# The order of the mixer's steps: a gated pair of products ahead of the first query products, the gates one product later

## The chip, the cores and the metric

One NeuronCore of a Trainium2 chip. The metric is the device time of one execution in microseconds, the median of several. TensorE (PE) does the matrix products, PEld are its weight loads, VectorE (DVE), ScalarE (ACT) and GpSimd (POOL) the elementwise work, and SyncE (SP) starts the transfers from HBM. Each engine takes its instructions from one queue in the order of the program.

## What is computed

Two layers of a decoder trunk on 512 tokens of 1024 features. Each has a mixer and an MLP, both with a conditioned normalisation ahead of them, and a normalised, gated residual behind them. The mixer, from the reference, shortened:

```python
u = h @ w_in
x_m, z, glu_a, glu_b = jnp.split(u, [1024, 2048, 3072], axis=-1)
x_c = silu(causal_depthwise_conv(x_m, w_conv_m, b_conv_m))       # 4 taps
q, k, v = headwise products of x_c, x_c, x_m                      # 4 heads of 256
ig, fg = split(concat(q, k, v) @ w_gates + b_gates)
h_m = mlstm_chunkwise(q, k / 16, v, ig, log_sigmoid(fg))
h_m = sigmoid(z) * group_layer_norm(h_m, 4 heads, g_mh)
a = causal_depthwise_conv(glu_a * sigmoid(glu_b), w_dw, b_dw)     # 31 taps
a = silu(group_layer_norm(a, 8 groups, g_cn, b_cn))
return concat(h_m, a) @ w_out
```

## The kernel before

Activations lie feature by feature: a tile is 128 features by 512 tokens. A float32 product is made of three passes in a reduced format (`passes`, L177 to L179): weight and activation are each split into a high and a low part. A weight block of 128 output features (`wblock`) is 512 KB; SP loads it, ScalarE casts the high part (L169), GpSimd subtracts for the low part (L170), and `gemm` makes 24 products of 512 columns from it into one of three PSUM banks "mm".

The mixer is written as steps, which `mixer` calls in the order of a string, `ORDERS[l]` for layer `l`:

- `Xh`: the two blocks of x_m of head h (`xm_proj`), and `Vh`, its 4-tap convolution and swish (`xm_conv`: ScalarE L525, L529, GpSimd L530, VectorE L533, then a cast L155 on ScalarE and a subtraction L156 on GpSimd). There is one buffer for the convolved tile.
- `Qh`: query, key and value products of head h (three blocks of 12 products; queries and keys read what `Vh` left), the transposes of the values (L567), and the head's share of the gates (six products L578, summed by VectorE at L583).
- `Gi`: gated tile i, two blocks (glu_b, then glu_a), ScalarE's tanh and VectorE's L438. Tiles 0 to 2 are made ahead of the string.
- `E`: the gates. Two products L591, L592 read the sum; a chain on ScalarE and VectorE (L601 to L612, scans L610 and L620, L622) follows, and its results are transposed on TensorE (L625, then L626) and spread into columns (L631, L636, L640).
- `Zi`: one block for the output gate. `ah`, `bh`, `ch`: scores, weighted sums and output of head h; a starts with a product L647 that spreads the running maximum, then score products L660 and VectorE's L652, L662; sums are L672, transposes L701.
- `Ci`: the 31-tap convolution of tiles 2i and 2i+1 (`conv31`): a first step L427 and 30 steps L429 each on VectorE, accumulating in PSUM. Then `conv_norm`: a copy by ScalarE (L476), four transposes (L479), statistics (L485, L486, L146), a scaling (L490), four transposes back (L494), and L500.
- `Oi`: the output projection's part of the convolved half. `Nj` (layer 0 only): conditioning products (L245, L250).

The string does not set the order on the engines by itself. The framework schedules: it issues ready instructions by priority, where an earlier place in the program counts as higher, and a timing model decides what is ready when. `Ci` stands late in the string, but its steps are issued earlier wherever that model finds VectorE free. The order found is then fixed in the program.

Of the kernel before, what the change touches and what calls it, by code (L numbers as in the profile page):

```python
# [53 lines left out]
def trunk(ctx, tc, xT, vecs, bg, cst, ccol, crow, wadn, wadt, win, win0, wqkv, wgate, wout, wff1, wff2, yT):  # L54
# [8 lines left out]
    ps = ctx.enter_context(tc.tile_pool(name="ps", bufs=1, space=PSUM))  # L63

    NSLOT = 25
    ORDERS = ['X0 G3 V0 X1 Q0 V1 N4 G4 X2 G5 N5 Q1 V2 X3 N6 Q2 V3 G6 Q3 E G7 N7 Z0 Z1 Z2 Z3 N8 a0 Z4 b0 Z5 a1 b1 Z6 N9 c0 C0 a2 Z7 c1 b2 C1 C2 C3 O0 O1 a3 O2 c2 O6 O3 b3 O4 O5 c3 O7', 'X0 V0 G3 X1 Q0 V1 X2 G4 Q1 V2 G5 X3 Q2 V3 G7 Q3 E Z0 G6 Z1 Z2 Z3 a0 Z4 Z5 b0 a1 Z6 b1 Z7 c0 a2 c1 C0 b2 C1 C2 C3 O0 O1 a3 O6 O2 c2 O3 b3 O4 O5 c3 O7']
    WPRI = 300
    NK = 4
    KM = 4
# [345 lines left out]
    def mixer(l, hp, pre):  # L415
# [309 lines left out]
        hm = []  # L725
        for step in ORDERS[l].split():
            i = int(step[1:] or 0)
# [173 lines left out]
```

## Time and profile before

| | us |
|---|---|
| median of three runs (1607.35 to 1611.52) | 1609.53 |
| the profiled execution, its own time | 1608.05 |
| its span | 1606.3 |
| TensorE busy | 1537.6 |
| VectorE busy | 878.1 |
| GpSimd busy | 798.5 |
| ScalarE busy | 688.6 |
| first product of X0, layer 0 (start) | 78.12 |
| first product of Z4, layer 0 | 301.53 |
| first product of Z4, layer 1 | 1064.80 |
| first product of O0, layer 1 | 1121.63 |

Layer 0's mixer begins at some 78 us, behind the conditioning and the first gated tiles; layer 1's at some 876 us. Busy times overlap, since the engines run beside each other; a wait in the profile names the engine and line that ended it. How rows are to be read is said with each group below.

### The profile page before, as it was taken

How to read it: one execution, taken by the hardware profiler on the slowest of the kernel's cores; microseconds unless marked ns; L12 is line 12 of the kernel's file. 1: busy time of each engine (PE TensorE's matmuls, PEld its weight loads, DVE VectorE, ACT ScalarE, POOL GpSimd, SP SyncE). 2: the span in 40 equal slices, each digit the busy share in tenths (PEclk: the TensorE clock that was granted, in tenths of full speed). 3: DMA queues.
4: the chain of work that ended last, by engine and by line, in shares of the span. 5: the costliest groups of instructions: out<-in, count | busy, mean ns of one | idle time of the engine just before them, and what ended most of it. 6: DMA issues, size and time to landing. Idle time of an engine off the chain costs nothing.

```text
span 1606.3 us, 21229 instructions
## 1 busy us (share of the span) xinstructions
PE 1537.6 (96%) x8020; PEld 1255.5 (78%) x8020; DVE 878.1 (55%) x1761; ACT 688.6 (43%) x1168; POOL 798.5 (50%) x488
## 2 busy tenths in 40 slices
PE   4899998999999999999999999999999999999997
PEld 3577665677998888888899777676899888888887
DVE  6399999843164432346747999997326320012114
ACT  3345563453454322332453665544355432233242
POOL 0166662256744444445962877434674444444462
PEclk9999999999999999999999999999999999999999
DMA  8514332413412555556730222220242233222331
GB/s 309 194 53 138 116 131 104 144 53 92 145 53 94 191 187 197 174 194 218 255 116 8 73 79 67 91 79 27 84 141 65 80 95 102 92 92 92 96 127 53
DMA packets 56270, 188.91 MB, mean 118 GB/s; under 512 B 6376, under 2 KB 8552, under 8 KB 56168
## 3 DMA queue, kind: packets, MB, share of 16 engines
q1 hardware_dynamic: 56168, 187.56, 35.2%
q8 instruction: 63, 1.03, 0.3%
q14 instruction: 39, 0.32, 0.1%
HBM read 185.44 MB, written 2.10 MB: 117 GB/s over the span
## 4 chain that ended last, share of the span: by engine, by line
PE 78%; DVE 6%; ACT 2%; POOL 1%; issue 1%; DMA 0%; POOLq 0%; ACTq 0%; DVEq 0%
PE ps_mm L177 23%; PE ps_mm L179 23%; PE ps_mm L178 23%; DVE ps_cv L429 3%; PE ps_mm L672 2%; PE ps_mm L660 2%; PE ps_ax L316 1%; PE ps_ax L245 1%; POOL wlo L170 1%; ACT whi L169 1%; PE ps_ax L578 1%; PE ps_ax L647 0%; DVE csb L490 0%; PE ps_ax L342 0%; PE ps_ax L701 0%
## 5 line engine op out<-in xcount | busy, mean ns | idle before, releaser
L170 POOL TENSOR_TENSOR wlo<-raw,whi 128x1024 fp32r<-128x1024 f32 (+1 forms) x216 | 498.8, 2311 | 565.1 <-ACT whi L169 547.0
L177 PE MATMUL ps_mm<-slot,whi 128*128 128x512 f32 (+1 forms) x1632 | 621.9, 382 | 8.1 <-ACT slot L155 4.9
L179 PE MATMUL ps_mm<-slot,wlo 128*128 128x512 f32 (+1 forms) x1632 | 622.1, 382 | 5.0 <-POOL wlo L170 4.8
L178 PE MATMUL ps_mm<-slot,whi 128*128 128x512 f32 (+1 forms) x1632 | 621.7, 381 | 0.0
L169 ACT CAST whi<-raw 128x1024 fp32r<-128x1024 f32 (+1 forms) x216 | 216.4, 1002 | 498.9 <-PE ps_mm L178 357.7
L177 PEld LDWEIGHTS ps_mm<-slot,whi 128*128 128x128 f32 x1632 | 307.3, 188 | 78.9 <-ACT slot L155 5.6
L179 PEld LDWEIGHTS ps_mm<-slot,wlo 128*128 128x128 f32 x1632 | 307.6, 188 | 73.8 <-issue 6.3
L178 PEld LDWEIGHTS ps_mm<-slot,whi 128*128 128x128 f32 x1632 | 308.0, 189 | 65.6 <-issue 3.8
L429 DVE SCALAR_TENSOR_TENSOR ps_cv<-slot,vv,ps_cv 128x512 f32<-128x512 f32 x480 | 332.9, 747 | 1.5
L767 DVE TENSOR_TENSOR ps_mm<-rl,ps_mm 128x512 f32<-128x512 f32 (+1 forms) x78 | 46.7, 599 | 280.6 <-ACT rl L766 280.5
L177 PE MATMUL ps_mm<-slot 128*128 128x256 f32 (+1 forms) x568 | 158.5, 292 | 14.5 <-DVE slot L769 7.4
L178 PE MATMUL ps_mm<-slot 128*128 128x256 f32 (+1 forms) x568 | 163.2, 290 | 0.3 <-POOL slot L355 0.3
L179 PE MATMUL ps_mm<-slot 128*128 128x256 f32 (+1 forms) x568 | 162.6, 289 | 0.0
L177 PEld LDWEIGHTS ps_mm<-slot 128*128 128x128 f32 x568 | 105.3, 190 | 19.9 <-ACT slot L357 8.4
L179 PEld LDWEIGHTS ps_mm<-slot 128*128 128x128 f32 x568 | 107.8, 190 | 2.2 <-issue 0.8
L178 PEld LDWEIGHTS ps_mm<-slot 128*128 128x128 f32 x568 | 107.6, 190 | 1.9 <-POOL slot L355 0.5
L170 POOL TENSOR_TENSOR slot<-raw,slot 128x1024 fp32r<-128x1024 f32 x34 | 85.2, 2527 | 14.4 <-issue 12.7
L272 DVE CUSTOM_DVE_ANT_0 adr<-adr,cbc,ini 128x1024 f32<-128x1024 f32 x40 | 66.0, 1659 | 23.3 <-DMA adr<-in_wadt 23.3
L147 POOL TENSOR_TENSOR small<-small,mhalf 128x4 f32<-128x4 f32 (+1 forms) x38 | 34.6, 911 | 81.3 <-DVE small L146 76.6
L769 DVE TENSOR_TENSOR slot<-ps_mm,slot 128x512 fp32r<-128x512 f32 (+1 forms) x78 | 46.4, 595 | 38.2 <-ACT slot L768 37.9
L530 POOL TENSOR_TENSOR xa<-xa,s 128x512 f32<-128x512 f32 x48 | 61.9, 1289 | 5.1 <-ACT s L529 1.9
L768 ACT CAST slot<-ps_mm 128x512 fp32r<-128x512 f32 (+1 forms) x78 | 39.8, 510 | 45.9 <-DVE ps_mm L767 45.9
(201 smaller groups left out, 1570.5 us busy)
## 6 DMA issues: line engine op xcount, KB each, us to landing
raw<-in_wff SPq DMA_DIRECT2D x138, 512.0 KB, 3.5
raw<-in_win SPq DMA_DIRECT2D x58, 512.0 KB, 3.3
adr<-in_wadt SPq DMA_DIRECT2D x56, 512.0 KB, 4.5
raw<-in_wout SPq DMA_DIRECT2D x36, 512.0 KB, 3.5
adr<-in_wadn SPq DMA_DIRECT2D x28, 512.0 KB, 4.2
raw<-in_wqkv SPq DMA_DIRECT2D x24, 256.0 KB, 2.6
slot<-in_wadt SPq DMA_DIRECT2D x8, 512.0 KB, 5.1
raw<-in_win SPq DMA_DIRECT2D x8, 384.0 KB, 7.1
```

The lines of the kernel that those rows point to most:

```text
L147: pool.tensor_tensor(y, u, mhalf[:, 0:n], op=ALU.pow)
L169: act.copy(out=r32(hi), in_=raw)
L170: (lo_eng or pool).tensor_tensor(r32(lo), raw, hi, op=ALU.subtract)
L177: pe.matmul(out, whi, xh, start=first, stop=False)
L178: pe.matmul(out, whi, xl, start=False, stop=False)
L179: mark[0] = pe.matmul(out, wlo, xh, start=False, stop=last)
L272: red = dve.tensor_tensor_reduce(raw, raw, cbc, scale, 0.0 if one else ini, ALU.mult, ALU.add, m)
L429: dve.scalar_tensor_tensor(acc, at[i][:, k:k + T], w, acc, op0=ALU.mult, op1=ALU.add)
L530: pool.tensor_tensor(acc, acc, tk, op=ALU.add)
L767: dve.tensor_tensor(o, rl[:, ts], o, op=ALU.mult)
L768: act.copy(out=r32(pr[:, 0, ts]), in_=o)
L769: last[0] = dve.tensor_tensor(r32(pr[:, 1, ts]), o, pr[:, 0, ts], op=ALU.subtract)
```

## The change

Only the two strings change. In both layers G4 now stands ahead of Q0, and the rhythm is X, G, Q, V for every head; G7 is ahead of Q3, and Z0 stands between Q3 and E. In layer 0 the conditioning steps N4 to N7 move one or two places with it; in layer 1 G6, which stood behind Z0, is now ahead of Q2. From Z1 (layer 0) and Z1 (layer 1) on, the strings are as before. The first part of each, cut behind Z3:

```diff
-X0 G3 V0 X1 Q0 V1 N4 G4 X2 G5 N5 Q1 V2 X3 N6 Q2 V3 G6 Q3 E G7 N7 Z0 Z1 Z2 Z3
+X0 G3 V0 X1 G4 Q0 V1 N4 X2 G5 Q1 N5 V2 X3 G6 Q2 N6 V3 G7 Q3 Z0 E N7 Z1 Z2 Z3
...
-X0 V0 G3 X1 Q0 V1 X2 G4 Q1 V2 G5 X3 Q2 V3 G7 Q3 E Z0 G6 Z1 Z2 Z3
+X0 V0 G3 X1 G4 Q0 V1 X2 G5 Q1 V2 X3 G6 Q2 V3 G7 Q3 Z0 E Z1 Z2 Z3
```

What the scheduler makes of it, at three places. First VectorE in layer 0, around the end of the gates' chain. Before, these rows stood there (L622 ends the chain, L500 ends a normalisation, L438 makes gated tile 7, L427 begins the convolution of the eighth tile):

```order
L429 SCALAR_TENSOR_TENSOR ps_cv<-slot,vv,ps_cv 128x512
L622 TENSOR_TENSOR s_1677<-s_1659,ml 4x512
L429 SCALAR_TENSOR_TENSOR ps_cv<-slot,vv,ps_cv 128x512
L500 SCALAR_TENSOR_TENSOR yt<-cth,ps_cx 128x512
L429 SCALAR_TENSOR_TENSOR ps_cv<-slot,vv,ps_cv 128x512
L438 SCALAR_TENSOR_TENSOR slot<-s_1735,ps_mm 128x512
L429 SCALAR_TENSOR_TENSOR ps_cv<-slot,vv,ps_cv 128x512
L427 TENSOR_SCALAR ps_cv<-slot,vv,hgb 128x512
```

Now gated tile 7 (its L438 is two rows further up) and the beginning of the eighth tile stand ahead of the last head's share of the gates (L583), with which the chain begins:

```order
L427 TENSOR_SCALAR ps_cv<-slot,vv,hgb 128x512
L429 SCALAR_TENSOR_TENSOR ps_cv<-slot,vv,ps_cv 128x512 x12
L485 BN_STATS small<-ps_cx 128x6 x4
L429 SCALAR_TENSOR_TENSOR ps_cv<-slot,vv,ps_cv 128x512
L486 BN_AGGR small<-small 128x2 x4
L429 SCALAR_TENSOR_TENSOR ps_cv<-slot,vv,ps_cv 128x512
L146 TENSOR_SCALAR small<-small 128x4
L429 SCALAR_TENSOR_TENSOR ps_cv<-slot,vv,ps_cv 128x512 x2
L490 TENSOR_SCALAR csb<-ps_cx,small 128x128 x4
L429 SCALAR_TENSOR_TENSOR ps_cv<-slot,vv,ps_cv 128x512 x2
L583 TENSOR_TENSOR gsb<-gsb,ps_ax 128x512
```

The eighth tile's first step has moved from behind the chain to ahead of its beginning. Counted over the whole queue from the first L427 of the layer, L427 and L429 stand 209 times ahead of L622 before and 248 times now (layer 1: 186 and 222).

Second, TensorE in layer 0, at the fourth tile's normalisation. Before, the transposes L479 stood among the key products of head 2, with other products up to L494:

```order
L178 MATMUL ps_mm<-slot,whi 128x512
L179 MATMUL ps_mm<-slot,wlo 128x512
L479 MATMUL ps_cx<-cs,csb 128x128 x4
L245 MATMUL ps_ax<-adr,cc 32x512 x2
L177 MATMUL ps_mm<-slot,whi 128x512
```

Now they stand between the two blocks of G6 (L250 belongs to the conditioning), and L494 follows directly:

```order
L179 MATMUL ps_mm<-slot,wlo 128x512
L250 MATMUL ps_ax<-cs,s_1220 128x1 x4
L479 MATMUL ps_cx<-cs,csb 128x128 x4
L494 MATMUL ps_cx<-cs,csb 128x128 x4
L177 MATMUL ps_mm<-slot,whi 128x512
```

The statistics and the scaling on VectorE lie between these two in the data, and no product stands between them any more.

Third, TensorE in layer 1, from the scores of the first head to Z4. Before, L647 and L626 stood among the products of Z1:

```order
L479 MATMUL ps_cx<-cs,csb 128x128 x4
L647 MATMUL ps_ax<-ml,cs 128x512
L179 MATMUL ps_mm<-slot,wlo 128x512
L177 MATMUL ps_mm<-slot,whi 128x512
L178 MATMUL ps_mm<-slot,whi 128x512
```

Now they stand behind Z3, and Z4 (the last row) comes behind the second L647, the last score products of the first head and the transposes of the seventh tile:

```order
L494 MATMUL ps_cx<-cs,csb 128x128 x4
L647 MATMUL ps_ax<-ml,cs 128x512
L626 MATMUL ps_ax<-cs,s_8748 128x4
L625 MATMUL ps_ax<-cs,s_8735 128x4
...
L631 MATMUL ps_ax<-tr,cs 128x16
L647 MATMUL ps_ax<-ml,cs 128x512
L660 MATMUL ps_mm<-slot 128x128 x2
L479 MATMUL ps_cx<-cs,csb 128x128 x4
L177 MATMUL ps_mm<-slot,whi 128x512
```

The blocks Z1 to Z3 are now ahead of L626, and no block of products stands between L626 and Z4.

## Rows read from the trace of the kernel before

**Rows 1.** The page: busy us (share); VectorE's 40 slices in tenths.

```profile
PE 1537.6 (96%) x8020; PEld 1255.5 (78%) x8020; DVE 878.1 (55%) x1761; ACT 688.6 (43%) x1168; POOL 798.5 (50%) x488
...
DVE  6399999843164432346747999997326320012114
```

**Rows 2.** Stretches: us, busy PE, PEld, DVE, ACT, POOL, clock, DMA, GB/s.

```profile
80.00:260.00 180.00, 168.79 (x778) 120.73 (x778) 174.03 (x300) 96.77 (x154) 111.03 (x89) 0.98 0.30 104
...
876.00:1040.00 164.00, 160.39 (x729) 121.74 (x728) 157.64 (x279) 97.99 (x156) 111.29 (x89) 1.00 0.24 76
```

**Rows 3.** VectorE by line, 78 to 270 us: count, busy, mean ns, idle.

```profile
L429 DVE SCALAR_TENSOR_TENSOR ps_cv<-slot,vv,ps_cv 128x512 f32<-128x512 f32 x202 | 138.8, 746 | 0.4
...
L490 DVE TENSOR_SCALAR csb<-ps_cx,small 128x128 f32<-128x128 f32 x24 | 8.1, 397 | 0.0
L485 DVE BATCH_NORM_STATS2 small<-ps_cx 128x6 f32<-128x128 f32 x24 | 5.3, 280 | 1.9 <-PE ps_cx L479 1.9
...
L146 DVE TENSOR_SCALAR small<-small 128x4 f32<-128x4 f32 x6 | 3.5, 586 | 0.0
```

**Rows 4.** VectorE's timeline, layer 0: start us, duration us, line, operation.

```profile
80.39 2.72 DVE L429 SCALAR_TENSOR_TENSOR ps_cv<-slot,vv,ps_cv 128x512 f32<-128x512 f32 x4
...
269.48 0.67 DVE L622 TENSOR_TENSOR s<-s,ml 4x512 f32<-4x512 f32 x1
```

**Rows 5.** Chain of waits, 205 to 262 us: shares by line.

```profile
by line: DVE ps_cv L429 52.9%; PE ps_ax L245 6.2%; issue 4.9%; DVE s L605 4.9%; DVE csb L490 4.5%; DVE xa L533 3.9%; PE ps_mm L179 2.4%; DVE s L610 2.2%; DVE gsb L583 2.1%; PE ps_mm L178 2.1%; DVE yt L500 2.1%; PE ps_mm L177 2.1%; PE ps_ax 
```

**Rows 6.** TensorE's waits, 78 to 356 us: total us, times, longest.

```profile
PE ps_mm L177 <- ACT slot L155: 4.9, 2, 3.5
PE ps_cx L479 <- ACT csb L476: 2.3, 1, 2.3
PE ps_mm L591 <- DVE gsb L583: 1.9, 1, 1.9
PE ps_ax L625 <- DVE s L612: 1.3, 1, 1.3
```

**Rows 7.** The page: subtraction, cast, transfer (us to landing). Timeline: two products.

```profile
L170 POOL TENSOR_TENSOR wlo<-raw,whi 128x1024 fp32r<-128x1024 f32 (+1 forms) x216 | 498.8, 2311 | 565.1 <-ACT whi L169 547.0
...
L169 ACT CAST whi<-raw 128x1024 fp32r<-128x1024 f32 (+1 forms) x216 | 216.4, 1002 | 498.9 <-PE ps_mm L178 357.7
...
raw<-in_win SPq DMA_DIRECT2D x58, 512.0 KB, 3.3
...
1042.12 0.39 PE L178 MATMUL ps_mm<-slot,whi 128*128 128x512 f32 x1
1042.35 0.39 PE L179 MATMUL ps_mm<-slot,wlo 128*128 128x512 f32 x1
```

**Rows 8.** TensorE's timeline, layer 0: first L626, L660, first of Z4.

```profile
277.48 0.22 PE L626 MATMUL ps_ax<-cs,s 4*128 4x4 f32 x1
...
295.37 4.14 PE L660 MATMUL ps_mm<-slot 128*128 128x512 f32 x12
...
301.53 0.50 PE L177 MATMUL ps_mm<-slot,whi 128*128 128x512 f32 x1 [0.25 <-DVE s L662]
```

**Rows 9.** Timelines, layer 1: L622; first L626, first of Z4.

```profile
1040.48 0.68 DVE L622 TENSOR_TENSOR s<-s,ml 4x512 f32<-4x512 f32 x1
...
1042.91 0.22 PE L626 MATMUL ps_ax<-cs,s 4*128 4x4 f32 x1
...
1064.80 0.48 PE L177 MATMUL ps_mm<-slot,whi 128*128 128x512 f32 x1
```

**Rows 10.** By line, whole run: ScalarE's copy of a convolved tile.

```profile
L476 ACT COPY csb<-ps_cv 128x512 f32<-128x512 f32 x16 | 9.4, 588 | 14.1 <-DVE ps_cv L429 14.1
```

**Rows 11.** TensorE's timeline and the table by stretch, layer 1, late.

```profile
1110.10 0.77 PE L660 MATMUL ps_mm<-slot 128*128 128x128 f32 x4 [1.42 <-DVE s L662]
...
1086.00:1122.00 36.00, 33.46 (x140) 24.25 (x139) 27.22 (x87) 16.90 (x37) 15.78 (x12) 0.91 0.09 30
```

**Rows 12.** Table by stretch, behind the wait at 112 us.

```profile
117.40:120.80 3.40, 3.40 (x9) 2.63 (x8) 3.40 (x6) 1.18 (x3) 3.32 (x4) 0.51 0.00 0
```

More of the change, by code (lines that the diff above doesn't have):

```diff
@@ L65, in trunk @@
     NSLOT = 25
-    ORDERS = ['X0 G3 V0 X1 Q0 V1 N4 G4 X2 G5 N5 Q1 V2 X3 N6 Q2 V3 G6 Q3 E G7 N7 Z0 Z1 Z2 Z3 N8 a0 Z4 b0 Z5 a1 b1 Z6 N9 c0 C0 a2 Z7 c1 b2 C1 C2 C3 O0 O1 a3 O2 c2 O6 O3 b3 O4 O5 c3 O7', 'X0 V0 G3 X1 Q0 V1 X2 G4 Q1 V2 G5 X3 Q2 V3 G7 Q3 E Z0 G6 Z1 Z2 Z3 a0 Z4 Z5 b0 a1 Z6 b1 Z7 c0 a2 c1 C0 b2 C1 C2 C3 O0 O1 a3 O6 O2 c2 O3 b3 O4 O5 c3 O7']
+    ORDERS = ['X0 G3 V0 X1 G4 Q0 V1 N4 X2 G5 Q1 N5 V2 X3 G6 Q2 N6 V3 G7 Q3 Z0 E N7 Z1 Z2 Z3 N8 a0 Z4 b0 Z5 a1 b1 Z6 N9 c0 C0 a2 Z7 c1 b2 C1 C2 C3 O0 O1 a3 O2 c2 O6 O3 b3 O4 O5 c3 O7', 'X0 V0 G3 X1 G4 Q0 V1 X2 G5 Q1 V2 X3 G6 Q2 V3 G7 Q3 Z0 E Z1 Z2 Z3 a0 Z4 Z5 b0 a1 Z6 b1 Z7 c0 a2 c1 C0 b2 C1 C2 C3 O0 O1 a3 O6 O2 c2 O3 b3 O4 O5 c3 O7']
     WPRI = 300
```

## The prediction

> **What bounds the kernel now.** I read the page's busy shares first. Over the whole run TensorE is busy 96% of the time and VectorE 55% [rows 1]. The slices of the same page show that this 55% is a mean over two kinds of stretch. In both mixers the VectorE digits are 8 or 9, and in the MLPs they fall to 4 and below. Table by stretch: VectorE works 174.0 of the 180 us from 80 to 260 (layer 0) and 157.6 of the 164 us from 876 to 1040 (layer 1), so it idles 6.0 and 6.4 us there [rows 2]. Most of it is the 31-tap depthwise convolution (138.8 us of the 192 from 78 to 270 [rows 3]): eight tiles a layer, 31 steps each, 248 steps a layer. Four steps in a row take 2.72 us from the start of the first to the end of the last, and one alone takes 0.75 on the mean, so a step costs (2.72 - 0.75) / 3 = 0.66 us of the queue [rows 4]. The small steps of the gates stand between such steps on VectorE's one queue, and the chain of waits from 205 to 262 us runs through convolution steps for 52.9% [rows 5]. So in that part of the mixer VectorE, not TensorE, sets the pace. TensorE's own waits in layer 0 are few: the four largest groups are 4.9 (query products, for the cast of the convolved tile), 2.3, 1.9 and 1.3 us [rows 6].
>
> **What the change does to the two queues.** TensorE's work is the same products in another order. The transfers, casts and subtractions of the weights move with their blocks: a block's 24 products, starting 0.23 us apart, take 5.5 us, its transfer lands in 3.3, its cast takes 1.0 and its subtraction 2.3 us [rows 7], and four gated or projection blocks in a row were served already (X0 and G3, ahead of G4 now). Those I cost at nothing. If that cover is gone (ScalarE held up), a block loses about 3.3 us, which is a rival below.
>
> The cost comes on VectorE. Gated tiles that are ready earlier let the scheduler place their convolution earlier, ahead of the gates' steps. In the order of the changed program 248 convolution steps stand ahead of L622 in layer 0 (209 before), and 222 in layer 1 (186 before). L622 is the last step of the gates' chain that TensorE waits for, at its first L626.
>
> **Layer 0, up to the first L626.** VectorE has 39 more steps ahead: 39 x 0.66 = 25.7 us. One more normalisation stands there (L485, L146 and L490, six of each so far: (5.3 + 3.5 + 8.1) / 6 = 2.8 us [rows 3]), and two more L500 and one L438, which I price at 0.7 each, like L622 [rows 4]. Together 30.6 us. TensorE has ahead of L626 in addition: Z2, Z3 and the last product of Z1, 49 x 0.23 = 11.3; the first eight score products, some 3.0 (twelve take 4.14 [rows 8]); twelve transposes, 1.3; less four conditioning products, 0.7. Together 14.9 us. Before, L622 ended at 269.48 + 0.67 = 270.15 [rows 4] and TensorE came to L626 at 277.48 [rows 8], with 7.3 to spare. So TensorE now waits, and is **30.6 - 14.9 - 7.3 = 8.4 us later** than the same progress before. Here the waits that the change is meant to remove (first query products and the rest) are swallowed: TensorE reaches the gates earlier, and waits longer there. The wait shows in pieces ahead of the gates: at the second transposes of the fourth normalised tile, which now follow the first ones directly between G6b and G6a, and around Q3, whose convolved input has 210 convolution steps ahead instead of 170.
>
> **Layer 0, from L626 to Z4.** Before, this took 301.53 - 277.48 = 24.0 us [rows 8]. Some 13 us of products have moved ahead, so 11 us would be left for TensorE. But the second L647 now stands ahead of Z4, and with it the first head's score chain and the last normalisation. I take 12.5, the length found for layer 1 below: **+1.5**.
>
> **Layer 1, up to L626.** 36 x 0.66 + 2.8 + 0.7 + 0.7 = 28.0 us more on VectorE. On TensorE 65 products (15.0), the first twelve score products (4.0) and four transposes (0.4), 19.4 us more. L622 ended at 1041.16 and L626 began at 1042.91 [rows 9], 1.75 to spare: **28.0 - 19.4 - 1.75 = +6.9**.
>
> **Layer 1, from L626 to Z4.** Before: 1064.80 - 1042.91 = 21.9 us [rows 9], of which 19.0 has moved ahead; TensorE alone would need 2.9. The transposes of the seventh tile now stand directly ahead of Z4, and behind L622 that tile has 14 convolution steps to go (9.2 us) and 13 short steps of the scores (2.1); the copy out takes 0.6 [rows 10] and the transposes 0.4. That is 12.3 us: **+9.4**.
>
> **Tails.** In layer 0 TensorE is full from Z4 on, before and now: 0. In layer 1 VectorE was late for TensorE by 1.42 us among the late convolution tiles, and the granted clock of 1086 to 1122 was 0.91, which lost 36 x 0.09 = 3.2 us [rows 11]. Now these tiles are done earlier: **-4.6**.
>
> **The sum** is 8.4 + 1.5 + 6.9 + 9.4 - 4.6 = +21.6 us. It is made against the profiled execution, 1608.05 us (its span 1606.3), which lies 1.5 below the median of three, 1609.53. Prediction: 1608.05 + 21.6 = 1629.65, **1630 us**.
>
> **Bounds.** What no row shows is how long VectorE will itself idle, waiting for TensorE or ScalarE. I kept the idle time of before. If it vanished, 6.0 + 6.4 = 12.4 us would come off: +9.2, 1617. If it doubled: +34.0, 1642. A long wait also lowers the clock: after the 3.5 us wait at 112 us, TensorE ran at a granted 0.51 (close to the lower level, 1.2 of 2.4 GHz) for 3.4 us [rows 12], 3.4 x 0.49 = 1.7 us lost. Where TensorE then waits again for VectorE that is free; behind the last wait, ahead of Z4 in each layer, it isn't. I count 0 in the sum and 3.4 at the upper end: 1645.
>
> **Rivals.**
>
> *Faster: TensorE alone decides.* At Q0 the two products of G4 (11.0 us) stand in the place of a 3.5 us wait, and with the waits at L155, L479, L591 and L625 gone the time falls by 4.9 + 2.3 + 1.9 + 1.3 = 10.4 us to about 1598. This decides if VectorE reaches L622 in layer 0 before TensorE does, at 277.48 + 14.9 - 10.4 = 282; by the sum above it gets there at 301, and without any idle time at 295. Convolution steps would have to cost about 0.58 us rather than 0.66. For it: the wait at Q0 surely goes, since the input has only 53 steps ahead. Against it: the steps come 0.66 apart wherever they stand in a row.
> The Trainium skill speaks for this rival: "Perfetto Trace Analysis", section "Identifying the Most-Contended Engine", calls the engine with the highest occupancy the one to improve and takes occupancy as a fair measure for VectorE. By the whole run's 55% VectorE would have room for any order, and only TensorE's idle time would count, about 1598. By the table by stretch it has 3% of room, so I weigh that result low. Chance 0.08.
>
> *No change.* VectorE's idle time goes, and the score chain ahead of Z4 is no longer than TensorE's own work there in layer 0 and half as long as I take it in layer 1: 21.6 - 12.4 - 1.5 - 4.7 = +3.0, 1611. For it: the idle time was partly caused by TensorE's own waits, which go. Chance 0.08.
>
> *Slower still: ScalarE's queue passes the delay on.* The copies of finished convolution tiles stand on ScalarE between the casts of the weights. If one waits for a late tile, the casts behind it, the subtraction on GpSimd (which already waits for casts most of the time [rows 7]) and the products wait too. Each of the eight tiles that meets this costs up to a cast and a subtraction, 3.3 us: three a layer give +20, about 1649. Against it: such a copy holds TensorE anyway, at the transposes that read it. Chance 0.06.
>
> That the change does not do what it says can be left out: in the order of the program G4 stands between X1 and Q0 in both layers, and the gates one product (Z0) behind Q3.
>
> **How the numbers follow.** The forecast has 0.78; its own range is 1617 to 1645. Two in ten may be left out: the range of 1612 to 1645 takes in its bounds and part of the case of no change. A measurement of this kernel tells some 0.3%, 4.8 us, from no change. Faster by more than that is the first rival (0.08). Within it lie the second (0.08) and a small part of the forecast: 0.09. Slower is the rest, 0.83.
>
> **What would show it.** In the profile after: TensorE's wait at the first query products is gone; in layer 0 new waits of several us for the convolution's copy or normalisation stand between G6b and G6a and before the Q3 products, together some 20 us up to the gates; L622 of layer 0 ends at about 301 us, and Z4 begins at about 313; in layer 1 TensorE waits some 8 us ahead of the first L626 and some 9 more at the seventh tile's transposes ahead of Z4; VectorE is as full as before up to the gates. The prediction is wrong if L622 ends before 290 us in layer 0, or if TensorE meets no wait over 3 us between G6 and Z4.

## The result and the profile after

The changed kernel took **1636.31 us**, the median of 5 runs (1635.47 to 1643.56), against 1609.53 before. The ratio is 1.0174, 95% interval 1.0158 to 1.0189: slower by 26.8 us, where 20.5 was forecast, and inside the range. The direction came out, and the size within the range. The runs below show that one cause was in the prediction and a second one was not.

The page of the profiled execution (1636.92 us, its span 1635.1), against [rows 1]:

```profile
PE 1543.9 (94%) x8020; PEld 1265.1 (77%) x8020; DVE 874.7 (53%) x1761; ACT 691.3 (42%) x1168; POOL 799.0 (49%) x488
```

The work is the same and the time is longer, so the shares fall. The table by stretch, against [rows 2]:

```profile
core 0: us, PE busy (x) PEld busy (x) DVE busy (x) ACT busy (x) POOL busy (x), PEclk, DMA share, GB/s
80.00:260.00 180.00, 156.10 (x715) 114.82 (x713) 170.03 (x311) 88.19 (x139) 104.95 (x85) 0.93 0.28 94
876.00:1040.00 164.00, 164.00 (x825) 132.84 (x824) 154.50 (x277) 91.63 (x153) 107.77 (x90) 1.00 0.21 68
```

In layer 0 VectorE now idles 10.0 us of the 180, where I had kept the 6.0 of before, so it waits for something itself. TensorE's waits from 78 to 356 us, against [rows 6] (columns: us in total, times, longest):

```profile
PE ps_cx L494 <- DVE csb L490: 10.2, 2, 9.1
PE ps_mm L177 <- ACT s L444: 6.1, 3, 2.6
PE ps_mm L177 <- ACT slot L155: 4.4, 1, 4.4
PE ps_cx L479 <- ACT csb L476: 1.6, 1, 1.6
```

The 9.1 us lie between G6b and G6a (198 to 207, b and a for glu_b's and glu_a's block), and most of the rest between 207 and 261, ahead of G6a and around the first products of Q3. At the gates themselves nothing is lost. The timeline, VectorE's row first, then two of TensorE's:

```profile
303.09 0.68 DVE L622 TENSOR_TENSOR s<-s,ml 4x512 f32<-4x512 f32 x1
...
305.10 0.22 PE L626 MATMUL ps_ax<-cs,s 4*128 4x4 f32 x1
...
319.48 0.80 PE L177 MATMUL ps_mm<-slot,whi 128*128 128x512 f32 x1
```

L622 ends at 303.8 (forecast 301). TensorE comes to L626 1.3 us later, without a wait. Z4's first product stands at 319.5, not at 313. In layer 1, from 1020 to 1125 us, two waits stand out; some 8 us ahead of the first L626 and 9 at the seventh tile's transposes were forecast:

```profile
PE ps_ax L647 <- DVE cols L640: 6.3, 1, 6.3
PE ps_ax L647 <- DVE ml L620: 6.2, 1, 6.2
```

The second line is the forecast wait ahead of L626. The first one stands at the second L647, for VectorE's L640, which has convolution steps ahead of it too; at the transposes L479 themselves only 0.8 us are left.

### The profile page after: what moved, and what is told of

Same layout as the page of the kernel before. It is cut to its first block, busy times and chain, and to the rows that moved or that the text cites. A ratio compares the mean times of both kernels' runs of the same rounds, so it can differ in the third digit from the quotient of the medians.

```text
span 1635.1 us, 21234 instructions
## 1 busy us (share of the span) xinstructions
PE 1543.9 (94%) x8020; PEld 1265.1 (77%) x8020; DVE 874.7 (53%) x1761; ACT 691.3 (42%) x1168; POOL 799.0 (49%) x488
## 4 chain that ended last, share of the span: by engine, by line
PE 87%; DVE 6%; ACT 2%; DMA 1%; POOL 1%; issue 1%; SPq 0%; POOLq 0%; ACTq 0%; DVEq 0%
PE ps_mm L177 26%; PE ps_mm L178 26%; PE ps_mm L179 26%; DVE ps_cv L429 2%; PE ps_mm L672 2%; PE ps_mm L660 2%; PE ps_ax L245 1%; PE ps_ax L316 1%; PE ps_ax L578 1%; DVE slot L272 0%; PE ps_ax L567 0%; DMA slot<-in_wadt 0%; POOL wlo L170 0%; PE ps_cx L494 0%; PE ps_cx L479 0%
## 5 line engine op out<-in xcount | busy, mean ns | idle before, releaser
L429 DVE SCALAR_TENSOR_TENSOR ps_cv<-slot,vv,ps_cv 128x512 f32<-128x512 f32 x480 | 331.7, 749 | 1.5
L177 PE MATMUL ps_mm<-slot 128*128 128x256 f32 (+1 forms) x568 | 159.9, 294 | 14.9 <-DVE slot L769 7.4
L177 PEld LDWEIGHTS ps_mm<-slot 128*128 128x128 f32 x568 | 106.4, 191 | 20.0 <-ACT slot L357 10.3
L179 PEld LDWEIGHTS ps_mm<-slot 128*128 128x128 f32 x568 | 108.9, 192 | 2.2 <-issue 0.8
L178 PEld LDWEIGHTS ps_mm<-slot 128*128 128x128 f32 x568 | 109.1, 192 | 1.7 <-POOL slot L355 0.3
```

The costliest lines, as they stand in the source:

```text
L177: pe.matmul(out, whi, xh, start=first, stop=False)
L178: pe.matmul(out, whi, xl, start=False, stop=False)
L179: mark[0] = pe.matmul(out, wlo, xh, start=False, stop=last)
L429: dve.scalar_tensor_tensor(acc, at[i][:, k:k + T], w, acc, op0=ALU.mult, op1=ALU.add)
```

## The experiments

Between the first X0 products of the two layers lie 797.6 us before and 816.8 after: layer 0 lost 19.2. The first four runs asked for each layer by itself, and for the mechanism of the prediction (**theory V**: late convolution steps ahead of the gates on VectorE).

**l0_only, l1_only.** One string of the change, the other as before.

> Layer 0 with the changed string, layer 1 with the old one. Theory (VectorE's one queue, each layer for itself): layer 0 alone gave +19 us between the layers' first X0 products in the profiles, so about 1628 us (1625 to 1632). Rival (what layer 0 loses is made worse by layer 1, or the delay travels on through weights, transfers and buffers): not additive, under 1622 or over 1634. Layer 1 should look as in the kernel before, X0 to O0 about 246 us.

> Layer 1 with the changed string, layer 0 with the old one. Theory: what the profiles show for layer 1 alone, +8 to +10 us, so about 1618 us (1616 to 1621), with the two waits of some 6 us at the first and the second L647. Rival (layer 1 only lost because layer 0 was late): within 1606 to 1613.

Measured: 1631.97 us (ratio to before 1.0131, 1.0109 to 1.0154) and 1619.66 (1.0061, 1.0046 to 1.0076). Both layers lose by themselves, 22.96 and 10.65 us. The sum, 33.6, is more than the change's 26.8. In l0_only the stretch from the first mixer's last projection to layer 1's X0 took 2.8 us more than in the changed kernel, and layer 1's mixer 4 us more than before, with the same orders; why is open.

**hold_last, b_hold_last.** The last two convolution tiles behind the gates, in the changed order and in that of before (`behind` sets the order of issue; `gl[0]` is the chain's last step, L640, a few steps behind L622).

```
-  dve.tensor_scalar(acc, at[i][:, 0:T], w, ...)
+  st_ = dve.tensor_scalar(acc, at[i][:, 0:T], w, ...); (i >= 6) and behind(st_, gl[0])
...
-  dve.tensor_tensor(cols[:, i, j, :], ...)
+  gl[0] = dve.tensor_tensor(cols[:, i, j, :], ...)
```

> The changed order, with the first convolution steps of the last two tiles (7th and 8th) held behind the last L622 of the gates on VectorE: in layer 0 64 steps fewer stand ahead of it than in the changed kernel (24 fewer than before), in layer 1 38 fewer (as before). Theory (steps of late tiles ahead of the gates' chain): VectorE reaches L622 of layer 0 some 40 us earlier, TensorE decides from there, the waits at L494, before Q3 and at L647 go, and the time falls from 1636 to about 1600 (1596 to 1608), below the kernel before. Rival A (the order on TensorE and ScalarE itself costs the time): stays at 1628 or more. Rival B (the held tiles are then late for the output products): the wait moves to the transposes of the last tiles ahead of O0, 1612 to 1628.

> Control: the order of before, with the same hold on the last two convolution tiles. 24 steps fewer ahead of L622 in layer 0, none fewer in layer 1. Theory: TensorE came to the first L626 after L622 in both layers, so little changes, 1603 to 1612. Rival (the hold is what helps by itself, whatever the order of the products): as low as the held changed order. Rival B of the run above: slower, 1613 to 1625.

Measured: **1648.68** (1.0239, 1.0222 to 1.0256) and 1608.83 (0.9991, 0.9979 to 1.0004). The first is a clear miss of theory V in layer 0. The stretch from 242 to 282 us, ahead of the gates, of hold_last and of the changed kernel:

```profile
242.00:282.00 40.00, 26.21 (x113) 18.01 (x111) 6.28 (x20) 18.24 (x30) 18.56 (x15) 0.79 0.29 102
```

```profile
242.00:282.00 40.00, 28.88 (x120) 19.12 (x119) 36.28 (x73) 22.41 (x36) 21.99 (x17) 0.79 0.29 100
```

VectorE works 6.3 us in place of 36.3 (third busy column), and the gates' first products (L591) begin at 282.6 instead of 280.7. With VectorE nearly empty TensorE still stood before Q3 (4.5 us for the cast of V): what was late came from elsewhere. The held steps then stood among the steps of the heads: between the gates and O0 TensorE waited 5.7 us for VectorE's L662 and L692 (0.7 in the changed kernel), and O0 began at 386.5 instead of 375.1. This is the slowest kernel of all. The control came out as expected.

**Theory N.** ScalarE's timeline of the changed kernel shows what Q3 waited for: the 4-tap convolution of V3. Its first tap (L525), then its other taps (L529) and the cast (L155) that the products read:

```profile
214.13 0.82 ACT L525 ACTIVATE xa<-xp,vv 128x512 f32<-128x512 f32 x1 [0.44 <-POOL slot L156]
...
241.68 0.78 ACT L496 ACTIVATE cth<-ps_cx,hgb 128x512 f32<-128x512 f32 x1 [5.36 <-PE ps_cx L494]
...
244.94 0.59 ACT L248 COPY s<-ps_ax 128x512 f32<-128x512 f32 x1 [0.56 <-PE ps_ax L245]
245.43 1.95 ACT L529 ACTIVATE s<-xp,vv 128x512 f32<-128x512 f32 x3
...
252.59 0.60 ACT L155 CAST slot<-xa 128x512 fp32r<-128x512 f32 x1
```

Before, first tap, row copy and other taps stood close together:

```profile
199.59 0.82 ACT L525 ACTIVATE xa<-xp,vv 128x512 f32<-128x512 f32 x1 [0.19 <-POOL slot L156]
...
204.18 0.59 ACT L248 COPY s<-ps_ax 128x512 f32<-128x512 f32 x1 [0.27 <-PE ps_ax L245]
204.67 1.95 ACT L529 ACTIVATE s<-xp,vv 128x512 f32<-128x512 f32 x3
```

In both kernels the taps follow directly on the row copy of N6 (L248). The taps, this copy and some other steps (the tanh of a gated tile, for one) take turns on five buffers, in the order in which the program names them, and the change puts N5 and N6 behind Q1 and Q2. So V3's taps now wait until TensorE has done Q2 and N6, 31 us after the first tap.

**l0_n_back, b_n, l0_g4.** Against layer 0's string (layer 1 as before): the change with N5 and N6 put back; the order of before with N5 and N6 alone moved; and with G4 alone moved.

```
change:     X1 G4 Q0 V1 N4 X2 G5 Q1 N5 V2 X3 G6 Q2 N6 V3 G7 Q3 Z0 E
l0_n_back:  X1 G4 Q0 V1 N4 X2 G5 N5 Q1 V2 X3 G6 N6 Q2 V3 G7 Q3 Z0 E
before:     X1 Q0 V1 N4 G4 X2 G5 N5 Q1 V2 X3 N6 Q2 V3 G6 Q3 E G7
b_n:        X1 Q0 V1 N4 G4 X2 G5 Q1 N5 V2 X3 Q2 N6 V3 G6 Q3 E G7
l0_g4:      X1 G4 Q0 V1 N4 X2 G5 N5 Q1 V2 X3 N6 Q2 V3 G6 Q3 E G7
```

> Layer 0 with the changed string, but N5 and N6 one step earlier again, ahead of Q1 and Q2 as before (layer 1 as before, so this stands against l0_only, 1632). New theory (N): V2's and V3's taps on ScalarE take their buffers behind N5's and N6's row copies, which the change put behind Q1 and Q2, so the inputs of Q2 and Q3 come late; with N5 and N6 back the waits of TensorE before Q3 and at the fourth tile's second transposes go or shrink below 3 us each, and the time is 1604 to 1615. Theory of the prediction (V: convolution steps ahead of the gates on VectorE): 243 steps instead of 251 stand ahead of L622, 8 x 0.66 = 5 us less, so 1625 to 1632.

> The order of before in both layers, with this part of the change alone: N5 behind Q1 and N6 behind Q2. Theory N: V2's and V3's taps come late as in the changed kernel, TensorE waits before Q2 and Q3, +8 to +20 us: 1617 to 1629. Theory V: 8 more convolution steps ahead of L622, 5.3 us, less than the 7.3 us that TensorE had to spare there: 1606 to 1612.

> The order of before, with this part of the change alone: in layer 0 G4 ahead of Q0. The convolution steps ahead of L622 stay at 209 and N5, N6 stay where they were. Theories N and V alike: the wait at Q0 (3.5 us) goes and nothing else comes, 1603 to 1609. Rival (an earlier gated pair costs by itself, through ScalarE's and GpSimd's queues): over 1613.

Measured: 1620.45 (1.0062, 1.0040 to 1.0084), **1637.56** (1.0177, 1.0149 to 1.0206) and **1606.03** (0.9980, 0.9968 to 0.9992). Moving two small conditioning steps costs 28 us by itself, as much as the whole change and some 9 more than the upper end that theory N gave; TensorE's largest wait group there is the cast of V:

```profile
PE ps_mm L177 <- ACT slot L155: 17.3, 4, 4.7
```

Putting them back gives 11.5 of layer 0's 23 us, less than theory N wanted (1604 to 1615), more than V. What remains in l0_n_back are two groups of waits for convolution tiles:

```profile
PE ps_cx L479 <- ACT csb L476: 9.3, 1, 9.3
PE ps_cx L494 <- DVE csb L490: 4.8, 3, 3.8
```

and there TensorE does wait for L622 at L626, as the prediction had it:

```profile
297.46 0.22 PE L626 MATMUL ps_ax<-cs,s 4*128 4x4 f32 x1 [0.91 <-DVE s L622]
```

G4 alone is a gain of some 3 us, about the 3.5 us wait at Q0 that it removes [rows 6]: of the parts that ran alone, the one that pays. The moves of G5 to G7, Z0 and E did not run alone.

**own.** Both strings of the change as they are, and one line:

```
-  rows = s2()
+  rows = scr.tile([P, T], F32, name="rows", tag="rows", bufs=1)
```

> The changed kernel in both layers, with one edit: the row copy of the N steps has a buffer of its own instead of one of the five that the taps of V take too. The strings, and so the order of the steps, stay the change's. Theory N (V2's and V3's taps come late because they take their buffers behind N5's and N6's copies): layer 0 gets back what putting N5 and N6 ahead of Q1 and Q2 gave it, 11 to 12 us (l0_only 1632, l0_n_back 1620.5), or a little more, layer 1 keeps its 10: 1620 to 1627. Rival (the place of the N products on TensorE costs the time, not the buffer): 1632 or more.

Measured: 1629.22 (1.0127, 1.0109 to 1.0145), 2 us above what N expected and below the rival's. In the profile layer 0 has 807.4 us between the X0 products, 9.4 less than the change and as much as with N5 and N6 put back (808.1). V3's second set of taps and its last cast now stand ahead of N6's copy on ScalarE:

```profile
203.25 1.94 ACT L529 ACTIVATE s<-xp,vv 128x512 f32<-128x512 f32 x3
...
224.51 0.62 ACT L155 CAST slot<-xa 128x512 fp32r<-128x512 f32 x1 [0.59 <-DVE xa L533]
231.56 0.59 ACT L248 COPY rows<-ps_ax 128x512 f32<-128x512 f32 x1 [2.47 <-PE ps_ax L245]
```

So sharing the buffers is what makes the place of N5 and N6 in the string costly. But with this one line the scheduler also finds another order, which the expectation leaves out. The fourth tile's transposes, in the changed kernel and in `own`:

```profile
197.25 0.63 PE L479 MATMUL ps_cx<-cs,csb 128*128 128x128 f32 x4
206.97 1.11 PE L494 MATMUL ps_cx<-cs,csb 128*128 128x128 f32 x4 [9.09 <-DVE csb L490]
```

```profile
200.07 0.63 PE L479 MATMUL ps_cx<-cs,csb 128*128 128x128 f32 x4
...
212.39 0.60 PE L494 MATMUL ps_cx<-cs,csb 128*128 128x128 f32 x4
```

In `own` other products stand between the two and the largest wait is gone, and 243 convolution steps instead of 248 stand ahead of L622 (242 in l0_n_back). From 78 us to the end of L622 VectorE works 206.3 us there and 214.2 in the changed kernel. So part of the 9.4 us comes through VectorE's queue and the order of TensorE; the runs do not separate this from the earlier taps. What stays are again waits for convolution tiles (8.0 and 5.1 us).

**l1_hold.** Layer 0 as before, the change in layer 1, with the hold of above there alone.

> Layer 0 as before, layer 1 with the changed string and the last two convolution tiles held behind the last L622 (186 steps ahead of it as before, 222 in l1_only, which took 1619.7). Theory V, for layer 1 alone, where there are no N steps: the two waits of some 6 us at L647 go and the time is 1608 to 1614. Rival (the order on TensorE costs it, whatever VectorE does): 1617 or more.

Measured: 1615.74 (1.0033, 1.0018 to 1.0047), 2 us above the band. Both waits at L647 are gone, and O0 comes 243.9 us after X0 (254.9 in l1_only). From O0 to the MLP's first product it then takes 62.2 instead of 55.6: of 11 us some 7 are given back. In layer 1 VectorE's late steps were the cause of these two waits, but holding two tiles back is no cure.

**b_half, n_back_half.** What is left of the loss against VectorE's load: `range(KDW)` becomes `range(16)` in the loop over the taps.

> The kernel before with 16 of the 31 taps of the depthwise convolution (taps 16 to 30 are left out of the result): 120 steps a layer fewer on VectorE, some 79 us a layer. It is the base of the next run. Theory V (VectorE's pace costs TensorE only small waits in the order of before): 1590 to 1606. Rival (VectorE holds nothing up before): 1607 or more.

> The changed strings with N5 and N6 of layer 0 ahead of Q1 and Q2, and 16 of the 31 taps, as in the run above (the same taps are left out). With all taps this order stands at +11 (layer 0, l0_n_back) and +10 (layer 1, l1_only) over before. Theory V (what is left of the loss is the convolution steps on VectorE's queue): with half of the steps the 21 us go, -8 to +4 against the run above. Rival (TensorE's, ScalarE's or GpSimd's order): +12 to +21 stay.

Measured: 1599.46 and **1596.35** (0.9938 and 0.9920 of before, intervals 0.9920 to 0.9955 and 0.9907 to 0.9933). The changed order, N5 and N6 apart, is now 3 us ahead where 21 behind was its sum with all taps. In n_back_half VectorE has room:

```profile
80.00:260.00 180.00, 178.31 (x822) 128.51 (x821) 134.32 (x261) 102.34 (x164) 116.57 (x93) 1.00 0.32 108
876.00:1040.00 164.00, 162.85 (x757) 125.22 (x756) 128.63 (x245) 103.04 (x164) 119.38 (x94) 1.00 0.24 78
```

and TensorE's longest wait from 78 to 356 us is 0.8. So the rest of the loss, beside N, goes with VectorE's load. (With fewer steps the scheduler also finds another order, 128 steps ahead of L622 in each layer, so this shows the load as the cause and not each single wait.)

**l0_g4_own.** The best order with the buffer of `own`.

> The fastest so far (the order of before with G4 of layer 0 ahead of Q0, 1606.0) with the same buffer of its own for the N copies. Theory N: V's taps no longer wait for any N, but in that order they hardly did: 1602 to 1607. Rival (earlier taps hold VectorE's and GpSimd's queues up elsewhere): 1608 to 1613.

Measured: 1608.73 (0.9996, 0.9987 to 1.0005): a miss, in the rival's range; no gain over before, and l0_g4's own 3 us are gone. I did not follow it up. **l0_g4 beats both kernels**, at 1606.03, by 0.2% over the one before.

## Why the prediction was right, and where it was not

- **VectorE bounds the mixers: right.** With half of the taps the changed order, N5 and N6 apart, costs nothing (3.1 us less than its base).
- **"The transfers, casts and subtractions of the weights move with their blocks ... Those I cost at nothing", with the N steps as 0.7 us of TensorE: the step that failed.** I listed N's products and not its copy on ScalarE, which shares buffers with V's taps. The term missing from layer 0 is some +9 (own) to +11.5 (l0_n_back), counted on top of the rest of the change. In the order of before it is +28 (b_n), so the two causes overlap and their shares do not add up.
- **The sum, +21.6.** Without N's part the two layers by themselves lose 10.9 (l0_n_back) and 10.7 (l1_only), together 21.6. The missing term took the change to 26.8, still inside the range. That the sum without N is met so exactly is partly luck, as the pieces show.
- **Layer 0, 8.4 + 1.5 = +9.9.** In l0_n_back (+10.9) TensorE reached L626 20.1 us later than before, counted from X0, with some 15.8 us of products more ahead of it: +4.3, not 8.4. The other 6 came behind L626. In the changed kernel it reached L626 27.9 us later with the 14.9 of the sum: +13.0, and +6.2 from there to layer 1's X0. The forecast wait between G6b and G6a came, but it went with N's buffer (9.1 us, none in `own`).
- **L622 in layer 0, forecast 301, measured 303.8.** VectorE from 78 us to the end of L622, before and after (us, busy, count, clock, DMA):

```profile
78.00:270.15 192.15, 186.07 (x333) 0.97 0.31 108
```

```profile
78.00:303.77 225.77, 214.22 (x386) 0.93 0.28 95
```

VectorE worked 28.2 us more, where the sum had 30.6, and idled 5.5 more, where the sum had kept the idle time of before. So the steps were there as counted, and the forecast was this close because two errors of opposite sign met.

- **Layer 1 up to L626, +6.9.** TensorE reached L626 187.8 us after X0, with 19.4 more work ahead than before, when it took 167.2: +1.2. The forecast wait came (6.2 us at L647), but VectorE was earlier than forecast: from X0's first product to the end of L622 it worked 182.9 us against 159.1 before, 23.8 more and not 28.0, and idled 4.8 against 6.4.
- **Layer 1 from L626 to Z4, +9.4:** 12.4 us against 2.9, so +9.5. The size was right and VectorE's queue set it, but most of the wait stood at the second L647 (6.3), not at the transposes (0.8).
- **Layer 1's tail, -4.6:** from Z4 to O0 53.4 us against 56.8, -3.4.
- **The rivals.** "TensorE alone decides" is out. "ScalarE's queue passes the delay on" had a chance of 0.06 and names the right engine, but not the way: its copies of convolution tiles (L476) wait 6.7 us for VectorE in layer 0 (78 to 356 us), against 9.5 before. What cost most on ScalarE was the order of buffers in front of V's taps.

## What to carry to other kernels

When a step is moved in an order, list every instruction that it issues on every engine, and every pool from which it takes a buffer: a copy of 0.6 us that shares five buffers with another step can hold that step back by all that stands ahead of the copy. A forecast by one engine's queue can hit the sum and miss the cause; empty that queue in an experiment and see whether the others come earlier. Try a change's parts alone: here one was worth -3 us and another +28 alone, but only +11.5 on top of the rest.

## What was not expected of the hardware

The clock after waits cost more than the 0 in the sum (the upper end of the range had 3.4). In the changed kernel, behind the 9.1 us wait and around Q3:

```profile
211.00:214.00 3.00, 3.00 (x8) 2.33 (x8) 3.00 (x6) 1.59 (x3) 1.21 (x1) 0.50 0.00 0
249.00:262.00 13.00, 4.48 (x10) 2.48 (x11) 12.39 (x29) 6.87 (x11) 7.38 (x8) 0.51 0.01 3
262.00:266.00 4.00, 4.00 (x11) 3.14 (x11) 4.00 (x7) 0.25 (x1) 1.17 (x1) 0.50 0.01 2
```

At a granted 0.50, the lower level of 1.2 GHz, TensorE is busy all of the 3 and 4 us, its products start 0.43 us apart instead of 0.23 [rows 7], and it does about half of its work: 3.5 us lost in these two stretches alone. Behind the second one TensorE meets no wait over 1 us up to Z4 that could swallow its part. At Z4, where the prediction said that such a stretch is not free, there is one in each layer: 0.50 from 320 to 324 us, behind several waits of under 1 us, and 0.57 from 1094.7 to 1100, behind the two of some 6 us. TensorE is busy throughout both. They lose 2.0 and 2.3 us (4.0 x 0.50 and 5.3 x 0.43).
